# A hybrid attention and RG-LRU layer on one core: one weight split moved ahead of another, and the attention gate's loads and sigmoids set further apart

## The chip, the cores and the metric

The kernel runs on one core of one Trainium2 chip. A core has a matmul engine (TensorE, PE in the trace, with its weight loads as PEld), a vector engine (DVE), a scalar engine (ScalarE, ACT), GpSimd (POOL) and SyncE (SP), which here issues nearly all DMAs. Each engine works through its own instructions in order and waits at semaphores for the others. The metric is the device time of one execution in microseconds, the median over several runs.

## The reference, cut to what matters

One layer of a decoder for 1024 prompt tokens and 32 sample tokens (8 sequences of 4), width 1024, all in float32:

```python
xn = rmsnorm(x, lw['norm1_g'])
proj = xn @ lw['w_in']
q, k, v, xr, gr, ga_logit, gr_logit = jnp.split(proj, IN_SPLITS, axis=-1)
...
att = window_attend(...)                      # 512 wide
xc, new_conv = causal_conv(xr, conv_prev, lw['conv_w'], lw['conv_b'])
h, h_last = rglru(xc, h0, ...)                # two 64x64 block products per block, a scan over time
rnn = (h.astype(x.dtype) * jax.nn.gelu(gr)) @ lw['w_o_rnn']
mix = (jax.nn.sigmoid(ga_logit) * (att @ lw['w_o_attn']) + jax.nn.sigmoid(gr_logit) * rnn) @ lw['w_out']
x = x + mix
hmid = jax.nn.relu(rmsnorm(x, lw['norm2_g']) @ lw['w_up'])
x = x + (hmid * hmid) @ lw['w_down']
...                                           # an input embedding behind a sigmoid gate
```

## The kernel before, in words

Everything is held transposed: 128 channels on the partitions, the 1056 tokens along the free dimension, cut into three chunks of 352 (`CH`). Each float32 product is made of three matmuls in a rounded 32-bit type: both operands are split into a high part (a cast) and a low part (the value less the cast), and `product` adds high by high, high by low and low by high, in this order. So the third matmul of a product is the first to read the weights' low part.

A product of 128 output channels is one call of `linear`, three chunks long. Weights come in the order of a queue `coming`. `fetch` issues the next load into one of two raw buffers; `divide` takes the oldest raw tile, splits it (L152: the cast `wh`, mostly on ScalarE; L153: the subtraction `wl`, mostly on the vector engine) and calls `fetch`, whose load waits until the raw buffer has been read. `weights` calls `divide` and hands out the oldest split pair, so a product's weights are split while the product before it runs. `wh` and `wl` have two buffers each.

`flow` sets the order of side work: `flow.run(gen, n)` starts a generator n chunks later, `yield n` continues it n chunks after, and `flow.step()` is called after each chunk. The order in which the program is written is the order on each engine's queue.

`recur(j)` runs once for each of 8 channel blocks. It has three `linear` products over the normalised input: the first group makes `xr`, the second `gr` (its gelu goes to `gl`), the third `ga_logit` (`sga`, stored to `a_dram`). The queue has a fourth weight in between, `rg`, the two block-diagonal weights of the recurrence, so the queue's order is first, second, `rg`, third. Between the products stand the convolution taps on the vector engine (L820, L821, in place in `xc`) and the generator `gates`, which starts one chunk into the second product. In `gates` the recurrent input `xc` is split into its parts `xhl` (two casts on ScalarE, one subtraction each on GpSimd and on the vector engine), a call of `divide` splits the third group's weights and `rg` is taken from `ready`; the block products, the sigmoids, the exponentials, the square root and the scan follow.

Then comes the attention output: for each of 8 blocks j, in the order `GA_ORDER`, `load_gate_a(j)` loads the stored logits back into the tile `A[j]` and takes their sigmoid on ScalarE, a `linear` over four blocks of the attention result (36 matmuls) multiplies `A[j]` chunk by chunk, and one block of the gated recurrence is split into `ra` and `rb_` for the next stage, the product with `w_o_rnn`. The tail of the last recurrence (square root, scan, product with `gl`) runs inside the first of these products. PSUM has four banks for the chunks of `linear`, so TensorE can run up to four chunks ahead of their evacuation.

The later stages (residual, `w_out`, the MLP by a Strassen-like scheme of seven products, the embedding gate) are not touched.

Of the kernel before, what the change touches and what calls it, by code (L numbers as in the profile page):

```python
# [20 lines left out]
KT = D // P  # L21
# [69 lines left out]
def trunk(ctx: ExitStack, tc: tile.TileContext, I, O):  # L91
# [3 lines left out]
    def f32(ap):  # L95
        return ap.bitcast(F32)
# [27 lines left out]
    def bank():  # L124
        return po.tile([P, 512], F32, tag="o", name="o")
# [6 lines left out]
    coming, raws, ready = deque(), deque(), deque()  # L132

    def fetch():
        if coming:
            load, split = coming.popleft()
            raws.append((load(), split))

    def divide():
        if raws:  # L140
            raw, split = raws.popleft()
            ready.append(split(raw))
            fetch()
# [60 lines left out]
    GA_ORDER = (5, 0, 6, 4, 1, 2, 3, 7)  # L204
# [34 lines left out]
    def linear(xk, nk, epilogue):  # L239
        w = weights()  # L240
        for c in range(3):
            piece(w, xk, nk, c, epilogue)
            flow.step()
# [82 lines left out]
    def col(name, j, n=1):  # L326
        return vec[:, vec_at[name] + j:vec_at[name] + j + n]
# [65 lines left out]
    def halves(g):  # L393

        return slice(g * HD, (g + 1) * HD), slice((1 - g) * HD, (2 - g) * HD)
# [404 lines left out]
    def recur(j):  # L800
        xr = big.tile([P, T], F32, tag="d6", name="xr")
        xsp = const1.tile([P, NB, 7], F32, tag="xsp", name="xsp", bufs=2)
        POOL.memset(xr[:, 0:3], 0.0)

        def put_xr(c, t0, n, ps):
            if c < 2:
                ACT.copy(xr[:, 3 + t0:3 + t0 + n], ps)
            else:
                ACT.copy(xr[:, 3 + t0:3 + NP], ps[:, :n - NS])
                ACT.copy(xsp[:, :, 3:], ps[:, n - NS:].rearrange("p (s t) -> p s t", t=NT))  # L810

        POOL.tensor_copy(xsp[:, :, 0:3], state[:, j, :24].rearrange("p (s w) -> p s w", w=3))
        linear(xnk, KT, put_xr)
        xc = big.tile([P, T], F32, tag="d0", name="xc")
        xcs = xc[:, NP:].rearrange("p (s t) -> p s t", t=NT)
        cw = lambda i: col("cw", i * KT + j)
        ACT.activation(xc[:, :NP], xr[:, 3:3 + NP], AF.Identity, scale=cw(3), bias=col("cb", j))
        ACT.activation(xcs, xsp[:, :, 3:7], AF.Identity, scale=cw(3), bias=col("cb", j))
        for i in range(3):
            DVE.scalar_tensor_tensor(xc[:, :NP], xr[:, i:i + NP], cw(i), xc[:, :NP], op0=ALU.mult, op1=ALU.add)  # L820
            DVE.scalar_tensor_tensor(xcs, xsp[:, :, i:i + NT], cw(i), xcs, op0=ALU.mult, op1=ALU.add)  # L821
        POOL.tensor_copy(state[:, j, 32:35], xr[:, NP:NP + 3])
        POOL.tensor_copy(state[:, j, 0:24].rearrange("p (s w) -> p s w", w=3), xsp[:, :, 4:7])
        gl = big.tile([P, T], F32, tag=f"e{j}", name="gl")

        def gates():
            xhl = [big.tile([P, T], F32R, tag=f"d{1 + 2 * b}", name="xhl") for b in range(2)]
            for b, low in enumerate((POOL, DVE)):  # L830
                o, other = halves(b)
                ACT.copy(xhl[b][o], xc[o])
                low.tensor_tensor(xhl[b][other], xc[o], f32(xhl[b][o]), op=ALU.subtract)
            yield 1
            divide()
            wh, wl = ready.popleft()
            yield 2
            rt = big.tile([P, T], F32, tag="d2", name="rt")
            it = big.tile([P, T], F32, tag="d4", name="it")
            for c, (t0, n) in enumerate(CH):  # L840
                t = slice(t0, t0 + n)
                for b in range(2):
                    o, other = halves(b)
                    ps = bank()[:, :n]
                    PE.matmul(ps, wh[:, b, :], xhl[b][:, t], start=True, stop=False)
                    PE.matmul(ps, wl[:, b, :], xhl[b][:, t], start=False, stop=True)
                    ACT.activation(rt[o, t], ps[o], AF.Sigmoid, bias=col("ba", j)[o])
                    ACT.activation(it[o, t], ps[other], AF.Sigmoid, bias=col("bx", j)[o])
                if c == 1:
                    yield 1  # L850
            a = big.tile([P, T], F32, tag="d7", name="a")
            a2 = big.tile([P, T], F32, tag="d1", name="a2")
            ACT.activation(a2, rt, AF.Exp, scale=nc16[:, j:j + 1])
            ACT.activation(a, rt, AF.Exp, scale=nc8[:, j:j + 1])
            ACT.activation(rt, rt, AF.Tanh, scale=pc8[:, j:j + 1])  # L855
            POOL.tensor_tensor(it, it, xc, op=ALU.mult)
            yield 1
            DVE.scalar_tensor_tensor(rt, a2, 1.0, rt, op0=ALU.add, op1=ALU.mult)  # L858
            yield 1
            ACT.activation(rt, rt, AF.Sqrt)  # L860
            DVE.tensor_tensor(rt, rt, it, op=ALU.mult)
            a0 = a[:, NP:].rearrange("p (s t) -> p s t", t=NT)[:, :, 0]
            b0 = rt[:, NP:].rearrange("p (s t) -> p s t", t=NT)[:, :, 0]
            ah = const1.tile([P, NB], F32, tag="ah", name="ah")
            DVE.tensor_tensor(ah, a0, state[:, j, 24:32], op=ALU.mult)
            DVE.tensor_tensor(b0, b0, ah, op=ALU.add)
            DVE.memset(a0, 0.0)
            DVE.tensor_tensor_scan(a, a, rt, 0.0, op0=ALU.mult, op1=ALU.add)
            yield 1
            POOL.tensor_copy(state[:, j, 35:36], a[:, NP - 1:NP])  # L870
            POOL.tensor_copy(state[:, j, 24:32], a[:, NP:].rearrange("p (s t) -> p s t", t=NT)[:, :, NT - 1])
            POOL.tensor_tensor(gl, a, gl, op=ALU.mult)
            rnn.append(gl)

        flow.run(gates(), 1)
        linear(xnk, KT,
               lambda c, t0, n, ps: ACT.activation(gl[:, t0:t0 + n], ps, AF.Gelu_apprx_tanh))

        st = stream.tile([P, T], F32, tag="st", name="sga")
        linear(xnk, KT,  # L880
               lambda c, t0, n, ps: ACT.copy(st[:, t0:t0 + n], ps))
        SP.dma_start(a_dram[j], st)
# [7 lines left out]
    def load_gate_a(j):  # L890
        A[j] = big.tile([P, T], F32, tag=f"d{j}", name="A")
        SP.dma_start(A[j], a_dram[j])
        ACT.activation(A[j], A[j], AF.Sigmoid)

    ra = big.tile([P, KT, T], F32R, tag="a", name="ra")
    rb_ = big.tile([P, KT, T], F32R, tag="b", name="rb_")
    load_gate_a(GA_ORDER[0])
    for i, j in enumerate(GA_ORDER):
        if i + 1 < KT:
            load_gate_a(GA_ORDER[i + 1])  # L900
        linear(lambda k: (qh[:, k, :], ql[:, k, :]), 4,
               lambda c, t0, n, ps: DVE.tensor_tensor(A[j][:, t0:t0 + n], A[j][:, t0:t0 + n], ps, op=ALU.mult))
        ACT.copy(ra[:, i, :], rnn[i])
        DVE.tensor_tensor(rb_[:, i, :], rnn[i], f32(ra[:, i, :]), op=ALU.subtract)

# [470 lines left out]
    for s in range(STEPS):  # L1376
# [8 lines left out]
        wh, wl = units[s // 2 * 2]  # L1385
# [82 lines left out]
    for th_ in range(2):  # L1468
        for j in range(KT):
# [8 lines left out]
            for c in range(2):  # L1478
                oc = slice(c * CQ, (c + 1) * CQ)
                ps = a[:, c, :CQ]  # L1480
                for k in range(KT):
                    wh, wl = gw[j][:, 0, k, :], gw[j][:, 1, k, :]
# [61 lines left out]
```

## Time and profile before

| what | value |
|---|---|
| median of 3 runs | 1647.29 us (1644.16 to 1647.4) |
| the profiled execution | 1645.6 us |
| its span, first to last instruction | 1643.8 us |
| TensorE busy (matmuls) | 1574.4 us, 96% |
| vector engine busy | 983.3 us, 60% |
| ScalarE busy | 810.6 us, 49% |
| GpSimd busy | 368.5 us, 22% |
| mean granted TensorE clock | 0.992 |

The profiled execution is one run of the program, a little below the median of the runs shown. Matmuls overlap in the engine, and the profile models their ends, so a matmul of 352 columns shows as 0.32 us long while the next one starts 0.16 us after it; where the argument needs TensorE's pace, it is taken from starts. The busy share of 96% is an average over stages; each stage has its own limit.

### The profile page before, as it was taken

To read this page: it belongs to the slowest core of one execution; us is meant where nothing else is said; L and a number is where in the kernel's file an instruction comes from. 1 tells how busy PE (TensorE), PEld (TensorE's weight loads), DVE (VectorE), ACT (ScalarE), POOL (GpSimd) and SP (SyncE) were. 2 spreads that over 40 slices of the span, in tenths; PEclk is the share of its full clock that TensorE was granted. 3 is DMA by queue.
4 is the path that set the end of the run, shared out by engine and by line. 5 is a ranking of instruction groups with operands and counts; after the bars stand their busy time and mean duration, and the time that the engine had idled before them with its cause. 6 is when DMAs were issued, how large, how long until landed. Compare 5 with 4: busy or idle time off the path is not lost.

```text
span 1643.8 us, 27541 instructions
## 1 busy us (share of the span) xinstructions
PE 1574.4 (96%) x11294; PEld 1551.5 (94%) x11294; DVE 983.3 (60%) x1352; ACT 810.6 (49%) x1295; POOL 368.5 (22%) x348
## 2 busy tenths in 40 slices
PE   6889999999999979999999999999999999999998
PEld 5889999999999968999999999999999999999997
DVE  6697655444444344332358888468846884689863
ACT  6555566666677652322235563445344534455442
POOL 4462225132222210223436120001000100012110
PEclk9999999999999999999999999999999999999999
DMA  5421112111211133334254793577357735790332
GB/s 176 64 94 59 63 66 69 55 56 56 70 57 56 46 99 109 104 104 130 79 193 175 267 201 105 209 286 131 105 209 287 129 107 208 288 179 1 98 93 75
DMA packets 170806, 203.69 MB, mean 124 GB/s; under 512 B 20500, under 2 KB 131268, under 8 KB 170664
## 3 DMA queue, kind: packets, MB, share of 16 engines
q1 hardware_dynamic: 153784, 185.15, 34.0%
q0 software_dynamic: 16896, 16.78, 6.8%
q8 instruction: 89, 1.46, 0.4%
q14 instruction: 37, 0.30, 0.1%
HBM read 150.78 MB, written 35.36 MB: 113 GB/s over the span
## 4 chain that ended last, share of the span: by engine, by line
PE 84%; DVE 6%; DMA 5%; ACT 3%; issue 2%; SPq 0%; ACTq 0%; DVEq 0%
PE acc L1392 13%; PE acc L1393 13%; PE acc L1391 13%; PE m L229 12%; PE m L227 12%; PE m L228 12%; DMA rev<-by_dist 2%; PE acc L1484 2%; PE acc L1486 2%; PE acc L1485 2%; DMA A<-a_dram 1%; DVE wl L153 1%; PE m L642 1%; PE o L630 1%; DVE qh L440 1%
## 5 line engine op out<-in xcount | busy, mean ns | idle before, releaser
L1393 PE MATMUL acc<-ring,wul 128*128 128x264 f32 x1792 | 511.8, 286 | 0.0
L1392 PE MATMUL acc<-ring,wuh 128*128 128x264 f32 x1792 | 510.3, 285 | 0.9 <-DVE ring L1183 0.9
L1391 PE MATMUL acc<-ring,wuh 128*128 128x264 f32 x1792 | 508.0, 284 | 0.6 <-ACT e L1362 0.5
L1391 PEld LDWEIGHTS acc<-ring,wuh 128*128 128x128 f32 x1792 | 338.0, 189 | 1.1 <-ACT e L1362 0.7
L1392 PEld LDWEIGHTS acc<-ring,wuh 128*128 128x128 f32 x1792 | 336.5, 188 | 1.3 <-DVE ring L1183 1.3
L1393 PEld LDWEIGHTS acc<-ring,wul 128*128 128x128 f32 x1792 | 336.5, 188 | 0.0
L229 PE MATMUL m<-xa,wl 128*128 128x352 f32 x912 | 296.1, 325 | 10.8 <-DVE wl L153 10.8
L227 PE MATMUL m<-xa,wh 128*128 128x352 f32 x912 | 298.0, 327 | 0.0
L228 PE MATMUL m<-xb,wh 128*128 128x352 f32 x912 | 295.4, 324 | 1.0 <-DVE xb L321 1.0
L229 PEld LDWEIGHTS m<-xa,wl 128*128 128x128 f32 x912 | 173.4, 190 | 12.9 <-DVE wl L153 12.9
L228 PEld LDWEIGHTS m<-xb,wh 128*128 128x128 f32 x912 | 173.4, 190 | 2.3 <-DVE xb L321 2.0
L227 PEld LDWEIGHTS m<-xa,wh 128*128 128x128 f32 x912 | 173.2, 190 | 1.0 <-ACT wh L152 0.3
L1148 ACT CAST wuh<-wblock 128x1024 fp32r<-128x1024 f32 x80 | 83.7, 1046 | 176.2 <-PE acc L1392 149.9
L1232 DVE TENSOR_TENSOR hid<-hid,acc 128x528 f32<-128x528 f32 x112 | 76.9, 700 | 84.0 <-PE acc L1393 57.1
L1232 DVE TENSOR_TENSOR X<-X,acc 128x528 f32<-128x528 f32 x156 | 104.6, 696 | 28.4 <-PE acc L1393 28.4
L1153 DVE TENSOR_TENSOR wul<-wblock,wuh 128x1024 fp32r<-128x1024 f32 x80 | 100.4, 1254 | 20.1 <-ACT wuh L1148 19.8
L153 DVE TENSOR_TENSOR wl<-wraw,wh 128x1024 fp32r<-128x1024 f32 (+1 forms) x61 | 70.7, 1169 | 65.5 <-ACT wh L152 65.1
L1112 POOL DMA_DIRECT2D wblock<-wblock x8 | 10.6, 1531 | 410.0 <-DMA wblock<-in_w_down 374.4
L1183 DVE TENSOR_TENSOR ring<-hid,ring 128x1056 fp32r<-128x1056 f32 x56 | 71.1, 1270 | 22.9 <-ACT ring L1182 22.9
L858 DVE SCALAR_TENSOR_TENSOR rt<-a,rt 128x1056 f32<-128x1056 f32 x8 | 10.1, 1258 | 119.8 <-ACT rt L855 119.8
L1182 ACT CAST ring<-hid 128x1056 fp32r<-128x1056 f32 x56 | 59.2, 1071 | 39.4 <-DVE hid L1170 14.0
L1484 PE MATMUL acc<-x2h,gw 128*128 128x264 f32 x256 | 74.6, 291 | 0.5 <-DVE gt L1454 0.5
(349 smaller groups left out, 3088.7 us busy)
## 6 DMA issues: line engine op xcount, KB each, us to landing
ring<-xc_dram SPq DMA_DIRECT2D x84, 528.0 KB
wblock<-in_w_down SPq DMA_DIRECT2D x40, 512.0 KB
wraw<-in_w_in SPq DMA_DIRECT2D x34, 512.0 KB
wblock<-in_w_up SPq DMA_DIRECT2D x32, 512.0 KB
xc_dram<-ring SPq DMA_DIRECT2D x28, 528.0 KB
wblock<-wblock POOLq DMA_DIRECT2D x16, 512.0 KB, 7.1
s<-wblock POOLq DMA_DIRECT2D x16, 512.0 KB, 5.6
s_dram<-sgr SPq DMA_DIRECT2D x8, 528.0 KB
```

The lines of the kernel that those rows point to most:

```text
L153: low.tensor_tensor(lo[:, :nk, :], raw[:, :nk, :], f32(hi[:, :nk, :]), op=ALU.subtract)
L227: PE.matmul(ps, wh, xh, start=k == 0, stop=False)
L228: PE.matmul(ps, wh, xl, start=False, stop=False)
L229: PE.matmul(ps, wl, xh, start=False, stop=k == nk - 1)
L1148: ACT.copy(units[u][0], w_view(ph_, PRODUCTS[q][0], p2))
L1153: DVE.tensor_tensor(lo, w_view(ph_, PRODUCTS[q][0], p2), f32(hi), op=ALU.subtract)
L1183: DVE.tensor_tensor(r[:, :, 1, :], src, f32(r[:, :, 0, :]), op=ALU.subtract)
L1232: put = lambda to, of, op: DVE.tensor_tensor(to, of, ps, op=op)
L1391: PE.matmul(ps, wh[:, k, m], r[:, 0, :], start=k == 0, stop=False)
L1392: PE.matmul(ps, wh[:, k, m], r[:, 1, :], start=False, stop=False)
L1393: PE.matmul(ps, wl[:, k, m], r[:, 0, :], start=False, stop=k == 3)
L1484: PE.matmul(ps, wh, xh, start=k == 0, stop=False)
```

## The change

It has two parts. In `gates`, the call of `divide` (which splits the third group's weights) and the taking of `rg` move from the chunk after the `xhl` split to just ahead of it, and the two waits of one and two chunks become one of three. In the attention output stage, `load_gate_a` only issues the load, and a new function `open_gate_a` takes the sigmoid. Loads are issued two tiles ahead instead of one; the sigmoid of the next tile stands behind the product of the present one, not ahead of it.

```diff
         def gates():
+            divide()
+            rg = ready.popleft()
             xhl = [big.tile([P, T], F32R, tag=f"d{1 + 2 * b}", name="xhl") for b in range(2)]
             for b, low in enumerate((POOL, DVE)):
                 o, other = halves(b)
                 ACT.copy(xhl[b][o], xc[o])
                 low.tensor_tensor(xhl[b][other], xc[o], f32(xhl[b][o]), op=ALU.subtract)
-            yield 1
-            divide()
-            wh, wl = ready.popleft()
-            yield 2
+            yield 3
+            wh, wl = rg
...
     def load_gate_a(j):
         A[j] = big.tile([P, T], F32, tag=f"d{j}", name="A")
         SP.dma_start(A[j], a_dram[j])
+
+    def open_gate_a(j):
         ACT.activation(A[j], A[j], AF.Sigmoid)
 
...
     load_gate_a(GA_ORDER[0])
+    load_gate_a(GA_ORDER[1])
+    open_gate_a(GA_ORDER[0])
     for i, j in enumerate(GA_ORDER):
-        if i + 1 < KT:
-            load_gate_a(GA_ORDER[i + 1])
+        if i + 2 < KT:
+            load_gate_a(GA_ORDER[i + 2])
         linear(lambda k: (qh[:, k, :], ql[:, k, :]), 4,
                lambda c, t0, n, ps: DVE.tensor_tensor(A[j][:, t0:t0 + n], A[j][:, t0:t0 + n], ps, op=ALU.mult))
+        if i + 1 < KT:
+            open_gate_a(GA_ORDER[i + 1])
         ACT.copy(ra[:, i, :], rnn[i])
         DVE.tensor_tensor(rb_[:, i, :], rnn[i], f32(ra[:, i, :]), op=ALU.subtract)
```

On ScalarE, in the second product of one turn of `recur` (here the seventh), the difference of the orders reads as follows; `gl` is the gelu of a chunk, `xhl` the two casts of the recurrent input, the first `wh` the third group's weights and the second `wh` the next turn's first group.

```order
 L877 ACTIVATE gl<-m 128x352
-L832 CAST xhl<-xc 64x1056 x2
-L877 ACTIVATE gl<-m 128x352
-L152 CAST wh<-wraw 128x1024
-L877 ACTIVATE gl<-m 128x352
+L152 CAST wh<-wraw 128x1024
+L834 CAST xhl<-xc 64x1056 x2
+L877 ACTIVATE gl<-m 128x352 x2
 L152 CAST wh<-wraw 128x1024
 L881 COPY sga<-m 128x352
```

The third group's cast has moved past the two `xhl` casts and one gelu.

On the vector engine the same place, behind the convolution taps:

```order
 L821 SCALAR_TENSOR_TENSOR xc<-xsp,vec,xc 128x32
-L833 TENSOR_TENSOR xhl<-xc,xhl 64x1056
-L153 TENSOR_TENSOR wl<-wraw,wh 128x1024 x2
+L153 TENSOR_TENSOR wl<-wraw,wh 128x1024
+L835 TENSOR_TENSOR xhl<-xc,xhl 64x1056
+L153 TENSOR_TENSOR wl<-wraw,wh 128x1024
 L858 SCALAR_TENSOR_TENSOR rt<-a_5213,rt 128x1056
```

The first of the two `wl` is the third group's, the other the next turn's first group's; the third group's has moved ahead of the `xhl` subtraction, right behind the last tap.

On ScalarE at the start of the attention output stage, from the last copy of `sga` on; L893 before and L895 after are the sigmoids of `A`, L152 the casts of the `w_o_attn` weights, L860 the square root of the last recurrence, L903 and L909 the cast `ra`. First before:

```order
L881 COPY sga<-m 128x352
L893 ACT_TABLE_LOAD
L893 ACTIVATE A<-A 128x1056 x2
L152 CAST wh<-wraw 128x512
L860 ACT_TABLE_LOAD
L860 ACTIVATE rt<-rt 128x1056
L903 CAST ra<-gl 128x1056
L893 ACT_TABLE_LOAD
L893 ACTIVATE A<-A 128x1056
L152 CAST wh<-wraw 128x512
```

And of the change:

```order
L881 COPY sga<-m 128x352
L895 ACT_TABLE_LOAD
L895 ACTIVATE A<-A 128x1056
L152 CAST wh<-wraw 128x512
L860 ACT_TABLE_LOAD
L860 ACTIVATE rt<-rt 128x1056
L895 ACT_TABLE_LOAD
L895 ACTIVATE A<-A 128x1056
L909 CAST ra<-gl 128x1056
L152 CAST wh<-wraw 128x512
```

One sigmoid instead of two stands ahead of the first cast, the second one stands behind the square root, and from then on the sigmoid of a turn's next tile stands behind that turn's weight cast; the number of table loads is the same. On SP three loads of `A` instead of two open the stage.

## Rows read from the trace of the kernel before

**Rows 1.** Span of the core and mean granted clock, the list of cores.

```profile
core 0: 1643.8 us, clock 0.992
```

**Rows 2.** TensorE's waits from 325 to 565 us: us in total, times, longest.

```profile
PE m L229 <- DVE wl L153: 10.8, 7, 1.7
```

**Rows 3.** TensorE's timeline around one wait: start us, us, instruction, idle before.

```profile
522.40 0.32 PE L228 MATMUL m<-xb,wh 128*128 128x352 f32 x1
524.25 0.43 PE L229 MATMUL m<-xa,wl 128*128 128x352 f32 x1 [1.53 <-DVE wl L153]
```

**Rows 4.** Windows, TensorE: length, busy (instructions), granted clock, DMA share, GB/s.

```profile
486.14:524.25 38.11, 36.58 (x228) 1.00 0.20 60
...
599.66:645.13 45.47, 39.04 (x216) 0.96 0.36 113
...
639.37:645.13 5.76, 5.76 (x36) 1.00 0.47 140
```

**Rows 5.** ScalarE's timeline in the second product of one `recur` turn.

```profile
514.81 0.47 ACT L877 ACTIVATE gl<-m 128x352 f32<-128x352 f32 x1
518.14 2.17 ACT L832 CAST xhl<-xc 64x1056 fp32r<-64x1056 f32 x2 [2.87 <-DVE xc L821]
...
520.83 1.05 ACT L152 CAST wh<-wraw 128x1024 fp32r<-128x1024 f32 x1
```

**Rows 6.** The vector engine's timeline there (the last row is two splits).

```profile
517.87 0.24 DVE L821 SCALAR_TENSOR_TENSOR xc<-xsp,vec,xc 128x32 f32<-128x32 f32 x1
520.35 2.60 DVE L833 TENSOR_TENSOR xhl<-xc,xhl 64x1056 fp32r<-64x1056 f32 x1 [2.24 <-ACT xhl L832]
522.97 2.36 DVE L153 TENSOR_TENSOR wl<-wraw,wh 128x1024 fp32r<-128x1024 f32 x2
```

**Rows 7.** GpSimd's timeline there.

```profile
519.36 2.47 POOL L833 TENSOR_TENSOR xhl<-xc,xhl 64x1056 fp32r<-64x1056 f32 x1 [2.66 <-ACT xhl L832]
```

**Rows 8.** SP's timeline there: three weight loads, the first at the start.

```profile
506.24 18.35 SPq L162 DMA_DIRECT2D wraw<-in_w_in  x3
```

**Rows 9.** Waits of all engines from 582 to 645.2 us.

```profile
ACT A L893 <- DMA A<-a_dram: 35.2, 8, 7.4
...
PE m L227 <- ACT wh L152: 12.8, 6, 7.1
```

**Rows 10.** ScalarE's timeline in the attention output stage.

```profile
585.65 1.08 ACT L893 ACTIVATE A<-A 128x1056 f32<-128x1056 f32 x1 [4.02 <-DMA A<-a_dram]
587.01 1.08 ACT L893 ACTIVATE A<-A 128x1056 f32<-128x1056 f32 x1 [0.28 <-DMA A<-a_dram]
588.00 0.60 ACT L152 CAST wh<-wraw 128x512 fp32r<-128x512 f32 x1
...
589.91 1.08 ACT L860 ACTIVATE rt<-rt 128x1056 f32<-128x1056 f32 x1
590.90 1.06 ACT L903 CAST ra<-gl 128x1056 fp32r<-128x1056 f32 x1
591.98 1.28 ACT L893 ACT_TABLE_LOAD   x1
595.23 1.09 ACT L893 ACTIVATE A<-A 128x1056 f32<-128x1056 f32 x1 [1.96 <-DMA A<-a_dram]
```

**Rows 11.** The vector engine's timeline there.

```profile
595.81 3.19 DVE L904 TENSOR_TENSOR rb__5581<-gl,ra 128x1056 fp32r<-128x1056 f32 x1
598.92 0.68 DVE L153 TENSOR_TENSOR wl<-wraw,wh 128x512 fp32r<-128x512 f32 x1
599.53 1.37 DVE L902 TENSOR_TENSOR A<-A,m 128x352 f32<-128x352 f32 x3
```

**Rows 12.** SP's timeline there: loads of `A` and of weights.

```profile
580.75 1.26 SPq L892 DMA_DIRECT2D A<-a_dram  x2
...
589.35 1.27 SPq L179 DMA_DIRECT2D wraw<-in_w_o_attn  x2
590.66 1.28 SPq L892 DMA_DIRECT2D A<-a_dram  x1
```

## The prediction

> **What bounds the kernel now.** The profiled execution took 1645.6 us, of which 1643.8 is the span [rows 1] and 1.8 lies around it; it stands 1.7 below the median of the three runs, 1647.29. I first looked for time in which TensorE waits, and found it near the change in two places.
>
> The first is the recurrence. Between 325 and 565 us the list of waits names one thing for TensorE: 7 waits on the vector engine's low-part split at L153 [rows 2]. The trace around one of them [rows 3] shows the matmuls 0.16 us apart up to 522.40, then nothing until 524.25. What is missing is the low part `wl` of the gate-logit weights (the third group, `w_in` columns from `OFF_GA`): the first two matmuls of a product need `wh` alone, the third needs `wl`. One turn of `recur` lasts 38.11 us and holds 228 matmuls at full clock [rows 4], which at 0.16 us would be 36.5: each turn loses one such wait and nothing else. The timelines say why it is late. ScalarE makes `wh` at 520.83, behind the two `xhl` casts that began at 518.14 [rows 5], though it had been free since 515.28 (514.81 plus 0.47) and waited 2.87 for the vector engine's convolution taps. The vector engine makes `wl` at 522.97, right behind its `xhl` subtraction of 520.35, which took 2.60 [rows 6].
>
> The second is the stage with the attention output product (`w_o_attn`). There 216 matmuls take 45.47 us [rows 4], where an undisturbed product of 36 takes 5.76, so 34.56 for six. TensorE waits 12.8 us on the copy `wh` at L152 and ScalarE, which makes that copy, waits 35.2 us for the loads of `A` [rows 9]. In each turn the load of the next `A` is issued only after that turn's weight load, which waits for the low split; its sigmoid stands ahead of the weight copy on ScalarE, so TensorE waits for the load by way of a sigmoid whose result it doesn't need yet. The longest of ScalarE's waits is 7.4 us.
>
> **The change, part by part.** *Third group's split.* No arithmetic is added. ScalarE's `wh` copy for the third group moves ahead of the `xhl` casts. Its raw weights were asked for at 506.24 [rows 8], 9 us earlier, so I take them as landed; the copy runs from 515.28 to 516.33, inside the 2.87 us in which ScalarE waits for the taps, so the casts stay at 518.14. The vector engine reaches `wl` when its last tap ends, 517.87 plus 0.24, and finishes it 1.22 later at 519.33. Its `xhl` subtraction can't start before 520.35 anyway, since it waits for ScalarE's second cast [rows 6]. So `wl` goes into a hole and is ready 3 us before TensorE wants it at 522.56 (522.40 plus 0.16). Each wait was 524.25 less 522.56, 1.69 us; seven make **11.8 us**. The list's 10.8 [rows 2] is the lower end, as it counts from modelled matmul ends. The eighth group, of the first turn, has no such wait in the list, and I give it nothing.
>
> What is late next? The recurrent matmuls need `xhl` after the first chunk of the third group: 24 matmuls behind 522.56, at 526.4, against 522.95 for the subtraction. Slack is 3.4 us. Behind the removed wait the rest of the turn is ordered by TensorE's chunks, so it moves with them. The next weights' load on SP moves earlier too, with the `wl` that frees its buffer.
>
> A subtraction on the vector engine can be held up by GpSimd, and the split moves next to one: GpSimd's `xhl` half ran from 519.36 for 2.47 us [rows 7], and the vector engine's half, begun at 520.35, ended 1.12 after GpSimd's did (522.95 against 521.83) instead of after its own length. The split, begun at 518.11, is ahead of 519.36 by 1.25 us, because GpSimd waits for a cast that itself waits for the same taps. The Trainium skill, "SBUF — State Buffer", section "Who interferes with whom", says that of a vector-engine instruction with two SBUF inputs and a GpSimd one that reads SBUF, the second to issue is fully blocked until the first is done; the row fits that. If the split came second, it would end 1.12 after 521.83, at 522.95, and leave 0.4 us of each wait: 8.8 us gained instead of 11.8.
>
> *Attention gate.* The first load and its sigmoid stay where they are (issue 580.75 [rows 12], sigmoid 585.65). Before, the second sigmoid came next at 587.01 and the weight copy at 588.00 [rows 10]; now the copy follows the first sigmoid at the same distance of 0.99, at 586.64. That moves it, and all that follows on ScalarE and the vector engine for the last recurrence (square root, scan, the first products, the subtraction at 595.81, the split at 598.92 [rows 11]), **1.36 us** earlier. The second sigmoid now stands behind the square root with its table load: 589.91 less 1.36, plus 1.09 for the root, 1.28 for the table, 1.08 for the sigmoid and 1.06 for the `ra` copy is about 593.1, still before the subtraction that needs `ra`, now 594.45.
>
> From the third product on (599.66 before, 598.30 now) I ask of each turn whether anything is later than 5.76 us. ScalarE has 0.60, 1.08 and 1.06 us of work [rows 10]; the vector engine 0.68, 1.37 and, counted with the hold-up by GpSimd that only the first one has, 3.19 [rows 11], so both fit. The loads: a load of `A` took 4.57 us from issue to sigmoid (590.66 to 595.23). Issued a turn earlier it has landed when the sigmoid comes up, the tightest being the fifth: its issue stands behind the two weight DMAs (1.27 us [rows 12]) that wait for the end of the split at 598.2, so it goes out at 599.5 and is there at 604.1; ScalarE comes to it after a weight copy that waits until TensorE has left its buffer, also about 604.1, and even 5 us later would do, since the product that multiplies it starts at 610. The weights themselves are split one product ahead, as before. So the six products run back to back: 45.47 less 34.56 is **10.9 us**.
>
> The loads cost something if three at once delay the first. In the trace the first of a pair had its sigmoid 4.90 us after issue (580.75 to 585.65), the second 1.36 after that. If the third shared equally, the first would be later by up to that 1.36; if they go in order, by nothing. One of the pair ended clearly ahead of the other, so I take nothing, and keep 1.4 for the range. The Trainium skill, "DMA: Bandwidth & Descriptors", section "Queues, rings and completion order", has the descriptors of one queue taken in ring order on each DMA engine, though not necessarily finished in order; by it the sum stays.
>
> Of the 45.47 us, part was at a lower clock (0.96 granted on average [rows 4], so about 1.8 us of it); the 10.9 takes the whole stage at full clock. A dip of the same size in the new stage would cost 1.8 back; that is the other upper bound.
>
> *After the stage* the order is unchanged: the output rows, the `sin` loads and the next weights hang on the end of the last product and move with it.
>
> *Sum:* 11.8 + 1.36 + 10.9 = 24.1 us; 1645.6 less 24.1 is 1621.5 for an execution like the profiled one. The shown median lies 1.7 above that one, so I put the median at 1622.5. Bounds for this case: 10.8 instead of 11.8, 1.4 for the loads, 1.8 for a clock dip and 1.7 for the spread of runs give 1627 at most; 1618.5 if the first turn gains too and the runs fall low.
>
> **Rivals.**
> *The wait in the attention stage stays* (7 in 100): the sigmoid still stands ahead of the next weight copy on ScalarE, so a late load would hold TensorE as before. For it speaks that every turn's load now hangs on the same chain; against it that a load has a turn of 5.76 and took 4.57. Then only 11.8 + 1.4 is gained: 1633.
> *The wait in the recurrence stays or is halved* (8 in 100). Halved, by GpSimd as above, 3.0 us are missing: 1625.5, inside the range (5 of the 8). Kept whole, by some order I misread: 1634.
> *Slower* (3 in 100): ScalarE's copy now stands ahead of the `xhl` casts and the second and third `gl` chunks, so raw weights that land late block them, and with them the recurrent matmuls. It costs nothing until it has used up 1.8 us (516.33 to 518.14) and the 3.4 us of slack, that is until a landing after 520.5, 14.3 us after the issue; beyond, each us costs 7. To eat the 24 us, it must be at 17.7. A load of nearly that size took 4.57 here, so this is far off. At 18.5, say, the time would be 1652. *No change* (2 in 100) is the same case near 17.7.
>
> **Numbers.** The forecast has 80 in 100. The range 1618 to 1630 holds it and the halved case. A change of 0.2%, 3.3 us, is about what this measurement can tell from none. The first three cases are all faster by more, 0.95 together; no change has 0.02 and slower 0.03.
>
> **What would show it.** In the profile after, the low-split wait of TensorE between 325 and 565 us is gone, and a turn of the recurrence is 36.5 us; the third group's `wl` starts right behind the last tap. In the attention stage ScalarE waits for a load of `A` once, some 4 us at the start, and the last six products take near 35 us. I am wrong if a wait of TensorE on L152 or L153 is left in these stages, if the weight copy waits for the raw load, or if the clock drops in the attention stage after the third product.

## The result and the profile after

The changed kernel takes 1620.7 us (median of 4 runs, 1619.52 to 1620.76) against 1647.26 (4 runs, 1644.16 to 1647.4): ratio 0.9841, 95% interval 0.9824 to 0.9859, so 26.6 us faster. Its profiled execution took 1620.71 us, practically the median; its span is 1618.9, against 1643.8 [rows 1].

The stretches show where the time came from. Both traces hold the same number of matmuls, so I cut them at the same ones: behind the 711th, still ahead of the change; in the last turn of the recurrence, at the matmul that waited for the low split before; and 409 matmuls later, in the first product with `w_o_rnn`. Windows of the kernel before (length, busy time and instructions of TensorE, PEld, the vector engine, ScalarE and GpSimd, granted clock, DMA share, GB/s):

```profile
0.00:150.29 150.29, 121.32 (x711) 113.98 (x712) 114.29 (x206) 83.19 (x182) 70.15 (x69) 0.97 0.38 100
150.29:562.38 412.09, 399.58 (x2544) 393.38 (x2542) 203.10 (x373) 274.04 (x500) 127.46 (x143) 1.00 0.19 60
562.38:650.80 88.42, 72.49 (x409) 68.34 (x410) 34.55 (x49) 39.74 (x48) 5.24 (x4) 0.94 0.31 97
650.80:1643.80 993.00, 981.00 (x7636) 975.84 (x7634) 631.39 (x726) 413.64 (x565) 165.60 (x132) 1.00 0.52 156
```

The same windows of the changed kernel:

```profile
0.00:148.91 148.91, 118.69 (x711) 111.12 (x712) 113.21 (x200) 83.21 (x182) 70.23 (x69) 0.99 0.38 100
148.91:548.60 399.69, 397.95 (x2541) 393.76 (x2542) 204.53 (x378) 272.90 (x499) 128.67 (x143) 1.00 0.20 63
548.60:624.71 76.11, 68.79 (x410) 67.56 (x410) 35.61 (x50) 40.73 (x50) 5.24 (x4) 0.96 0.36 109
624.71:1618.90 994.19, 980.49 (x7636) 974.53 (x7634) 631.71 (x726) 413.47 (x565) 166.10 (x132) 1.00 0.52 156
```

The recurrence lost 12.4 us, the attention output stage 12.3. The two ends, where the program is the same, differ by 1.4 us one way and 1.2 the other.

In the recurrence TensorE has no wait left between 325 and 555 us, where the list showed 7 on the low split [rows 2]. ScalarE's timeline in the turn of [rows 5], now:

```profile
504.51 0.47 ACT L877 ACTIVATE gl<-m 128x352 f32<-128x352 f32 x1
504.87 1.04 ACT L152 CAST wh<-wraw 128x1024 fp32r<-128x1024 f32 x1
507.82 2.17 ACT L834 CAST xhl<-xc 64x1056 fp32r<-64x1056 f32 x2 [1.91 <-DVE xc L821]
```

And the vector engine's, beside [rows 6]:

```profile
507.55 0.24 DVE L821 SCALAR_TENSOR_TENSOR xc<-xsp,vec,xc 128x32 f32<-128x32 f32 x1
507.71 1.21 DVE L153 TENSOR_TENSOR wl<-wraw,wh 128x1024 fp32r<-128x1024 f32 x1
510.03 2.60 DVE L835 TENSOR_TENSOR xhl<-xc,xhl 64x1056 fp32r<-64x1056 f32 x1 [1.11 <-ACT xhl L834]
```

The copy `wh` took 1.04 us out of the wait for the taps, which shrank from 2.87 to 1.91; `wl` stands right behind the last tap and takes its own length, 1.21; the `xhl` subtraction still waits for ScalarE and is as long as before. Both moved pieces fill holes.

In the attention output stage the waits of all engines, 565 to 640 us, are the counterpart of [rows 9]:

```profile
ACT wh L152 <- PE m L228: 18.9, 6, 5.1
...
PE m L227 <- ACT wh L152: 5.5, 1, 5.5
...
ACT A L895 <- DMA A<-a_dram: 3.8, 1, 3.8
...
PE m L229 <- DVE wl L153: 1.6, 1, 1.6
...
PE m L227 <- DVE A L906: 0.2, 1, 0.2
```

Apart from the stop of 5.5 us at the start, TensorE no longer waits for ScalarE's weight copy, as it did six times before; ScalarE waits for TensorE to leave the weight buffer instead, and for one load of `A` where it was eight. ScalarE's timeline, beside [rows 10]:

```profile
571.51 1.08 ACT L895 ACTIVATE A<-A 128x1056 f32<-128x1056 f32 x1 [3.77 <-DMA A<-a_dram]
572.50 0.60 ACT L152 CAST wh<-wraw 128x512 fp32r<-128x512 f32 x1
...
589.78 0.62 ACT L152 CAST wh<-wraw 128x512 fp32r<-128x512 f32 x1 [5.12 <-PE m L228]
590.31 1.08 ACT L895 ACTIVATE A<-A 128x1056 f32<-128x1056 f32 x1
```

One sigmoid stands ahead of the first weight copy; from then on each sigmoid finds its tile landed.

### The profile page after: what moved, and what is told of

Same layout as the page of the kernel before. It is cut to its first block, busy times and chain, and to the rows that moved or that the text cites. A ratio compares the mean times of both kernels' runs of the same rounds, so it can differ in the third digit from the quotient of the medians.

```text
span 1618.9 us, 27541 instructions
## 1 busy us (share of the span) xinstructions
PE 1565.9 (97%) x11294; PEld 1547.0 (96%) x11294; DVE 985.0 (61%) x1352; ACT 810.3 (50%) x1295; POOL 370.2 (23%) x348
## 4 chain that ended last, share of the span: by engine, by line
PE 84%; DVE 8%; ACT 3%; DMA 3%; issue 1%; SPq 0%; DVEq 0%; ACTq 0%
PE acc L1398 13%; PE acc L1399 13%; PE acc L1397 13%; PE m L227 12%; PE m L229 12%; PE m L228 12%; DMA rev<-by_dist 2%; PE acc L1490 1%; PE acc L1492 1%; PE acc L1491 1%; PE m L642 1%; PE o L630 1%; DVE qh L440 1%; DVE hn L253 1%; DVE hn L254 0%
## 5 line engine op out<-in xcount | busy, mean ns | idle before, releaser
L153 DVE TENSOR_TENSOR wl<-wraw,wh 128x1024 fp32r<-128x1024 f32 (+1 forms) x61 | 71.2, 1168 | 46.4 <-ACT wh L152 46.2
```

The lines of the kernel that those rows point to most:

```text
L153: low.tensor_tensor(lo[:, :nk, :], raw[:, :nk, :], f32(hi[:, :nk, :]), op=ALU.subtract)
```

## The experiments

Unless said otherwise, an edit is made to the changed kernel.

**The two parts alone.** One kernel has only the edit of `gates`, the other only that of the attention gate (the two halves of the diff above).

> Only the first part of the change: the third group's weight split ahead of the recurrent input's parts; the attention stage as in the kernel before. My theory: the seven waits of TensorE on the low split between 325 and 565 us go, 1.7 to 1.8 us each, and nothing else moves: 12 to 13 us less than before, about 1635. A turn of the recurrence takes 36.3 us. Rival (the gains are not separate: part of the time won here is won only because the attention stage behind it no longer waits for loads): less than 9 us are gained.

> Only the second part: loads of the attention gate two tiles ahead, sigmoid behind the product; the recurrence as before. My theory: the attention stage loses 12 us, so about 1635, and this and the first part alone add up to the whole change within 1.5 us. Rival (the earlier loads only profit from the shorter recurrence, or the reverse): the two parts add up to clearly more or clearly less than the whole.

Measured beside 1645.39 us for the kernel before: 1635.41 for the split alone (ratio 0.9936, 0.9924 to 0.9949), 1633.94 for the gate alone (0.9935, 0.9922 to 0.9948). Windows of five turns of the recurrence and of the stage behind, the split alone:

```profile
370.22:551.88 181.66, 181.66 (x1141) 181.66 (x1141) 82.63 (x81) 130.97 (x186) 59.56 (x55) 1.00 0.20 60
551.88:639.90 88.02, 71.85 (x411) 67.78 (x410) 35.05 (x50) 40.71 (x50) 5.22 (x4) 0.94 0.31 95
```

The gate alone:

```profile
370.53:561.16 190.63, 183.02 (x1140) 181.57 (x1140) 82.71 (x81) 130.53 (x185) 59.55 (x55) 1.00 0.19 58
561.16:637.27 76.11, 68.90 (x409) 67.67 (x410) 35.08 (x49) 39.77 (x48) 5.21 (x4) 0.96 0.37 112
```

By stretches the parts are separate: five turns take 181.7 us with the edit and 190.6 without, the stage 76.1 with it and 88.0 to 88.4 without, each whatever the other part is. The medians add up less well: 9.98 and 11.45 us, 21.4 together, against 26.6 for the whole. So the expectation that they add up within 1.5 us holds for the stretches the edits touch and not for the medians, and the split alone missed its 12 to 13 us by the median, though not by the stretch. Of the 5.1 us that are missing, 1.9 is the kernel before, whose median was 1647.26 beside the whole and 1645.39 here. Another part lies ahead of the change: the profiled execution of the split alone had run its first 711 matmuls by 152.59 us, at a mean granted clock of 0.94, the kernel before by 150.29 at 0.97, with the same program up to there. In the twelve profiles of this document these 711 matmuls, the same code in each, took 148.5 to 152.6 us. How much of it is in the other executions, no trace shows.

**Which half of the gate's edit counts.** First the loads stay two ahead and each sigmoid goes back ahead of the product:

```diff
     open_gate_a(GA_ORDER[0])
+    open_gate_a(GA_ORDER[1])
     for i, j in enumerate(GA_ORDER):
         if i + 2 < KT:
             load_gate_a(GA_ORDER[i + 2])
+        if 0 < i and i + 1 < KT:
+            open_gate_a(GA_ORDER[i + 1])
...
-        if i + 1 < KT:
-            open_gate_a(GA_ORDER[i + 1])
         ACT.copy(ra[:, i, :], rnn[i])
```

> The changed kernel, with the loads still two tiles ahead but each sigmoid put back ahead of the product before it, so ahead of the next weight copy on ScalarE. My theory (the load's distance is enough once it is a whole turn): a sigmoid finds its tile landed, ScalarE waits for no load but the first two, and the time is that of the changed kernel plus the 1.4 us of the second sigmoid ahead of the first weight copy: 1621 to 1623. Rival (the sigmoid's place is what counts): TensorE waits again for weight copies in each turn, and most of the 11 us of the six later products is lost: above 1628.

Then the sigmoid stays behind the product and the loads go back to one ahead:

```diff
-    load_gate_a(GA_ORDER[1])
     open_gate_a(GA_ORDER[0])
     for i, j in enumerate(GA_ORDER):
-        if i + 2 < KT:
-            load_gate_a(GA_ORDER[i + 2])
+        if i + 1 < KT:
+            load_gate_a(GA_ORDER[i + 1])
```

> The changed kernel with the loads of the attention gate one tile ahead again and only the sigmoid behind the product. My theory (the place of the sigmoid alone would have been enough, since a load issued in one turn then has until the next turn's first multiplication, over 7 us, while it takes some 4.6): no wait of TensorE comes back in the six later products and the time is that of the changed kernel, 1620 to 1622. Rival (the load's distance is needed, because a sigmoid that waits for its load also holds the ra copy and the next weight copy): ScalarE is late by some us in each turn and the time is above 1624.

Measured: 1622.63 us for the first (ratio to the kernel before 0.9862, 0.9848 to 0.9875), 1621.67 for the second (0.9846, 0.9832 to 0.9859). The window of the stage, the first's and then the second's:

```profile
548.64:626.34 77.70, 68.03 (x410) 66.80 (x410) 35.59 (x50) 41.28 (x50) 5.22 (x4) 0.96 0.35 107
```

```profile
549.45:625.49 76.04, 68.73 (x411) 67.50 (x410) 35.69 (x50) 41.24 (x50) 5.23 (x4) 0.96 0.36 109
```

Two rows of ScalarE's timeline, of the second:

```profile
590.15 1.09 ACT L895 ACTIVATE A<-A 128x1056 f32<-128x1056 f32 x1 [6.64 <-DMA A<-a_dram]
...
599.34 1.09 ACT L895 ACTIVATE A<-A 128x1056 f32<-128x1056 f32 x1 [2.33 <-DMA A<-a_dram]
```

And two of the waits of the first, from 548 to 627 us:

```profile
ACT A L895 <- DMA A<-a_dram: 12.1, 6, 5.5
...
PE m L227 <- ACT wh L152: 7.1, 1, 7.1
```

Each half alone brings nearly all: 76.04 and 77.70 us, where the stage takes 76.11 with both and 88.42 before. With one load ahead ScalarE still waits for loads in the later turns, once for 6.6 us and then for up to 2.3, but behind that turn's weight copy, and TensorE's waits in the stage are those of the changed kernel within 0.1 us (5.4 on the first copy, 1.6 on a low split, 0.3 on a multiplication). With the sigmoid ahead ScalarE waits for loads six times, against my expectation of the first two alone, but TensorE's waits for weights are the same two as in the changed kernel, the first of them 7.1 us instead of 5.5: that is the second sigmoid ahead of the first weight copy, priced at 1.36 in the prediction; the stage is 1.6 longer. The later weights are split a product ahead, and that lead takes the delays up. The loop before was slow only because both held: the load late and the sigmoid in front.

**The split issued while GpSimd subtracts.** The call of `divide` goes between the two halves of `xhl`:

```diff
-            divide()
-            rg = ready.popleft()
...
                 low.tensor_tensor(xhl[b][other], xc[o], f32(xhl[b][o]), op=ALU.subtract)
+                if b == 0:
+                    divide()
+                    rg = ready.popleft()
```

> The changed kernel, with the third group's split put between the two halves of the recurrent input's parts: behind ScalarE's first cast and GpSimd's subtraction, ahead of the second cast. The vector engine's low split is then issued while GpSimd's subtraction of 2.47 us runs. Theory of blocking (a subtraction of the vector engine issued second waits until GpSimd's has ended): the split ends about 1.2 us after GpSimd's end however early it was issued, some 0.4 us of each wait come back, and the kernel is about 3 us slower than the changed one, 1623 to 1624.5. Rival (the two engines only slow each other, or don't meet): the split takes at most twice its length of 1.22 from its issue, and either nothing of the wait comes back (1621), or the row of the split shows no stretched duration.

Measured 1624.19 us, against 1620.7 and 1621.3 for the changed kernel, which was measured twice. GpSimd's and the vector engine's rows:

```profile
511.32 2.47 POOL L833 TENSOR_TENSOR xhl<-xc,xhl 64x1056 fp32r<-64x1056 f32 x1 [2.66 <-ACT xhl L832]
```

```profile
512.17 2.71 DVE L153 TENSOR_TENSOR wl<-wraw,wh 128x1024 fp32r<-128x1024 f32 x1 [2.09 <-ACT wh L152]
```

The split lasted 2.71 us instead of 1.21 and ended 1.09 after GpSimd's end (514.88 against 513.79). That is blocking, as expected: it lasted longer than twice its own length, the most that the rival allowed. Five turns take 184.12 us, 0.49 more in each, so 3.4 over seven, near the 3.0 that the prediction gave this rival.

**What is left at the start of the stage.** TensorE stops for 5.8 us and then for 0.6 and 1.9. Four steps, each on top of the one before it (the definitions of the two functions, which step 1 moves ahead of `recur`, are left out):

```diff
# 1: loads ahead of the last store
+        if j == KT - 1:
+            load_gate_a(GA_ORDER[0])
+            load_gate_a(GA_ORDER[1])
         SP.dma_start(a_dram[j], st)
...
-    load_gate_a(GA_ORDER[0])
-    load_gate_a(GA_ORDER[1])
     open_gate_a(GA_ORDER[0])
# 2: the first sigmoid in the evacuation of the first chunk
-    open_gate_a(GA_ORDER[0])
...
+            if i == 0 and c == 0:
+                open_gate_a(j)
# 3: the last tail later
-    GA_ORDER = (5, 0, 6, 4, 1, 2, 3, 7)
+    GA_ORDER = (5, 0, 6, 3, 1, 2, 4, 7)
...
-            yield 1
+            yield 1 if j < KT - 1 else 4
             ACT.activation(rt, rt, AF.Sqrt)
# 4: and in three pieces
+            if j == KT - 1:
+                yield 3
             DVE.memset(a0, 0.0)
             DVE.tensor_tensor_scan(a, a, rt, 0.0, op0=ALU.mult, op1=ALU.add)
-            yield 1
+            yield 1 if j < KT - 1 else 3
```

> The changed kernel with its first two loads of A issued ahead of the store of the last sga tile on SP instead of behind it. They then wait only for the recurrence's last block product, some 5 us earlier. My theory (the 5.8 us gap of TensorE at the start of the attention stage is the latency of the first load, which stands behind that store): ScalarE finds the first tile landed when its last sga copy is done, does the table load and the sigmoid, and copies the weights some 3.8 us earlier; about 1617. Rival (the gap is bound by ScalarE's chain of the last recurrence, not by the load): under 1 us is gained.

> As the kernel with the early loads, and the first sigmoid of the attention stage moved behind the first weight copy too (into the evacuation of the first chunk). TensorE can then run one chunk further before it needs the first multiplication for a free bank. My theory: 1 to 2 us less than with the early loads alone, 1615 to 1616, since the square root and the scan of the last recurrence still stand between the first and the second multiplication on the vector engine. Rival (the weight copy was not what held TensorE, the banks were): no difference.

> As the kernel before it, and the last recurrence's tail (square root, scan, product on GpSimd) three chunks later, into the second product, with the order of the gate tiles changed to 5, 0, 6, 3, 1, 2, 4, 7 so that no load needs a tile that the tail still reads. My theory: the vector engine multiplies the first three chunks and splits the next weights at once, and both gaps of TensorE at the start of the stage (5.8 and 1.9 us, with the low clock between them) go almost wholly: 1610 to 1613. Rival (the tail's work only moves its waits into the second and third product): not below 1615.

> As the kernel with the tail three chunks later, with that tail also spread: the square root and its product in the second attention product, the scan in the third, GpSimd's product in the fourth. In the kernel before it the vector engine had product, scan and a subtraction held up by GpSimd in one turn, and TensorE waited 0.9 and 1.9 us. My theory: spread out, each piece fits beside the turn's own 3.3 us of work in 5.8, both waits go, and some 2.5 us are gained: about 1612. Rival (the vector engine has no slack left after the stage's late start): the waits only move to a later product, 1614 to 1615.

Measured medians: 1615.83, 1617.0, 1614.82 and 1613.14 us; the last has ratio 0.9796 to the kernel before (0.9781 to 0.981). The same stretch of 409 matmuls that takes 76.1 us in the changed kernel takes 72.36, 73.02, 68.94 and 67.22. TensorE's waits in it, and the window of its stops, step 1:

```profile
PE m L227 <- DVE A L907: 2.3, 1, 2.3
PE m L227 <- ACT wh L152: 1.7, 1, 1.7
PE m L229 <- DVE wl L153: 1.6, 1, 1.6
```

```profile
568.43:582.00 13.57, 7.79 (x43) 6.63 (x43) 10.27 (x14) 12.72 (x14) 2.76 (x3) 1.00 0.44 138
```

Step 2, with the granted clock of the window behind its wait:

```profile
PE m L227 <- DVE A L909: 4.0, 1, 4.0
```

```profile
575.00:582.00 7.00, 5.78 (x20) 5.71 (x21) 7.00 (x9) 4.67 (x7) 2.72 (x3) 0.51 0.18 72
```

Step 4, its wait and the stretch:

```profile
PE m L229 <- DVE wl L153: 0.8, 1, 0.8
```

```profile
548.06:615.28 67.22, 66.32 (x410) 65.32 (x410) 35.30 (x50) 40.64 (x50) 5.23 (x4) 1.00 0.41 124
```

Step 1 gains as expected, 3.7 us of the stretch: of the stop of 5.8 us, 3.8 were the wait for the first load behind the last store, and 2.0 are left. Step 2 missed, and its rival was right: it took the wait for the weight copy away, TensorE ran on to the matmul of step 1's second stop, the 143rd of the stretch, and stood there for 4.0 us until the second multiplication gave a bank free, since square root and scan lie between the first and the second. That matmul starts 27.7 us into the stretch in both steps, so the weight copy did not set the time to it; the chain of square root, scan and multiplication did. With that one long stop came a window at 1.2 GHz (0.51); step 1's stretch ran at full clock (1.00), and so do those of steps 3 and 4. Step 4 left one wait: GpSimd's product ran as soon as the scan was done and again held up a subtraction (rows in the last section), so placing it later in the program did not place it later in time. Steps 3 and 4 came in at 1614.8 and 1613.1 where 1610 to 1613 and about 1612 were expected.

**The changed kernel again**, beside step 4:

> The changed kernel once more, for a direct comparison beside the kernel with the spread tail. My theory: 1619.5 to 1621; a turn of the recurrence takes 36.3 us and the six later attention products 35 us, whatever the first 150 us of the execution do. Rival (the differences of 1 to 2.5 us between sum and medians come from the changed stretches): these two lengths differ by over 0.5 us from those of the first profile.

Measured 1621.3 us (ratio 0.9847, 0.9834 to 0.986) beside 1646.79, 0.3 above the expected range; step 4 is about 8 us faster. Five turns take 181.67 us as in the first profile, the stage 76.17 against 76.11, the six later products 34.96 in both.

## Why the prediction was right

1620.7 came out where 1622.5 was forecast, and the two mechanisms are those it named: each part removes the waits that it was meant to remove, by the piece that was moved.

- *The split in the hole:* as told, piece by piece. The term was 11.8 us, the stretch lost 12.4. A turn takes 36.33 us where I worked out 36.5 at 0.16 us a matmul, against 38.12 before: each wait cost 1.79, not 1.69. The wait itself is the 1.69 of the forecast; the sum left out that the matmul behind it also cost 0.10, since the next one started 0.26 after it and not 0.16 (524.25 in [rows 3], and the row behind it):

```profile
524.51 0.32 PE L227 MATMUL m<-xa,wh 128*128 128x352 f32 x1
```

- *The first turn* gained nothing, as assumed: TensorE's stop for the sample attention there is 2.0 us in both profiles.
- *GpSimd's hold-up as a rival:* not met in the changed kernel, since the split is issued first. Issued second it costs 3.4 us by the run, against 3.0. The 3.0 is itself a slip: 0.39 us of each of seven waits (522.95 less 522.56) makes 2.7, so 9.1 us would have been left and not 8.8.
- *The attention gate:* 1.36 and 10.9 us, together 12.3; the stretch lost 12.3. That the total agrees so well is partly luck, for each term is off by 0.4. The stretch ahead of the six later products (562.38 to 599.66 before, 548.60 to 584.14 now) lost 1.7, of which 0.2 is the load below. The six products take 34.96 us, against the 45.47 of [rows 4], so they lost 10.5: they run without a wait, but at 5.83 each and not at the 5.76 of one undisturbed product.

```profile
584.14:619.10 34.96, 34.96 (x217) 34.88 (x218) 20.75 (x33) 12.84 (x15) 0.00 (x0) 1.00 0.45 135
```

- *Three loads at once:* the first had its sigmoid 4.66 us after issue (566.85 to 571.51), against 4.90 with two [rows 10, 12], so the third did not delay it, and the end I took for the sum was right.
- *The clock:* at full in the later products, and the low stretch at the start stayed. No dip came back, so the 1.8 us kept for one were not needed.
- *The reason behind the gate's gain* was incomplete: I gave both the distance of the load and the place of the sigmoid, and the runs show that either alone would have been nearly enough (77.70 and 76.04 us for the stage, against 76.11).
- *A sign of being wrong* was written too widely: a wait of TensorE on L152 or L153 left in these stages. Two are left, 5.5 and 1.6 us, both at the start of the attention stage, where the kernel before has them too (7.1 and 1.6). None is left in the stretches that the sum counted as won.
- *From the sum to the median:* I added 1.0 because the kernel before was profiled 1.7 below its median. The changed kernel's profile lay on its median, so the sum, 1621.5, was the better number. The two stretches account for 24.7 us and the two profiled executions for 24.9; the rest of the measured 26.6 is in executions of the same code: the kernel before had medians of 1645.4 to 1647.3 in the measurements here, and the first 150 us differed by 1.4 us between the two profiles.

Whether the 1.2 us that the last 990 us took longer is an effect of the change stays open. There is one profile of the kernel before, with 993.0 us; the eleven of kernels with an edit have 993.4 to 995.0. All eleven have one or two short waits of the output transposes on the vector engine after 1490 us (0.3 to 1.7 us in all; 0.9 in the changed kernel) which the one before lacks.

## What to carry to other kernels

When an engine in the middle of a chain sits idle for one input, look for work behind it on its queue that has its own inputs already and that the engine that sets the time will want: here two operations of about 1 us moved into holes of 2.9 and 2.2 us, and nothing else moved. An operation that waits for a late load should not stand ahead of an operation that the engine that sets the time waits for. Here ordering the waiter behind it did the same as loading earlier (76.04 us for the stage against 77.70).

## What was unexpected of the hardware

The clock did not fall with every stop of TensorE. With the stop of 5.8 us in the changed kernel (567.35 to 573.15) and that of 4.4 us in step 2 (571.85 to 576.22) came a stretch at half clock. In step 1 three stops of 2.0, 2.6 and 1.9 us, from 568.43 to 581.46, passed at full clock (1.00 in the window shown above), while in the kernel before a stop of 2.2 us (620.37 to 622.59), the last of three of over 1 us between 605 and 623 us (1.7, 1.2 and 2.2), was followed by one:

```profile
623.40:626.90 3.50, 3.50 (x13) 3.50 (x14) 2.33 (x4) 0.12 (x1) 0.00 (x0) 0.51 0.50 128
```

What it costs is seen in the changed kernel: matmuls start 0.29 us apart instead of 0.16, 18 in 5.39 us.

```profile
573.15:578.54 5.39, 5.39 (x18) 5.16 (x19) 4.07 (x7) 5.35 (x5) 0.00 (x0) 0.50 0.32 72
```

In step 4 a later place in the program did not put GpSimd's product later in time. GpSimd had been idle for 18.4 us, and its product ran right behind the scan, which ended at 581.78, and two short copies; the vector engine's subtraction took 3.17 us instead of 1.25:

```profile
582.12 2.48 POOL L883 TENSOR_TENSOR gl<-a,gl 128x1056 f32<-128x1056 f32 x1
```

```profile
582.54 3.17 DVE L917 TENSOR_TENSOR rb__5585<-gl,ra 128x1056 fp32r<-128x1056 f32 x1
```
